# Two token groups run ahead in the opening of a two-layer mixer step on one Trainium2 core

## The chip, the core and the metric

The kernel runs on one core of one Trainium2 chip. Its five engines work side by side and wait for each other through semaphores: TensorE (PE; its weight loads are listed as PEld), VectorE (DVE), ScalarE (ACT), GpSimd (POOL) and SyncE (SP), which issues the transfers. The metric is the time of one execution on the device, in microseconds (us); lower is better.

## The reference

One inference step of a two-layer backbone over 1152 tokens (128 context, 1024 latent) with 1024 channels. Each layer normalises and modulates its input, multiplies it with one combined input weight, runs windowed attention and a pooling mixer beside each other, gates both, multiplies with an output weight and adds the result to the residual. Cut to what matters here:

```
silu_c, silu_ctx = silu(c), silu(c_ctx)
for l in range(2):
    shift, scale, gate = split(silu_c @ w_ada[l] + b_ada[l], 3)   # context tokens: silu_ctx
    h = rmsnorm(x) * norm_w[l] * (1 + scale) + shift
    q, k, v, ga, u, gp = split(h @ w_in[l])       # 512 128 128 512 512 512 columns
    q, k = rope(q), rope(k)                       # latent tokens alone
    a = rmsnorm(attention(q, k, v, cache)) * silu(ga)
    p = rmsnorm(pool_mixer(u)) * silu(gp)
    x = x + gate * (concat(a, p) @ w_out[l])
y = rmsnorm(x)                                    # k and v of the context are returned too
```

## The kernel before

**Layout.** Everything lies transposed: 128 channels on the partitions, tokens along the free dimension. The tokens are in three groups (g = 0, 1, 2) of 384; group 0 holds the 128 context tokens and the first 256 latent ones, which have modulations of their own, so that its modulation steps go in two parts (128 and 256 columns). `G[g]` holds a group's 8 channel blocks in fp32. `H[g]` holds the modulated input as two parts, hi and lo, whose sum is the fp32 value.

**A projection tile** (`project`, called by `job`) is 128 output columns of one group: for each of 8 channel blocks three matmuls (weight hi with H hi, weight hi with H lo, weight lo with H hi), 24 in all, into one PSUM accumulator. The weight's column is loaded raw in two halves (`wload`), ScalarE rounds it to hi and another engine subtracts to get lo (`wsplit`); the pair lies in one of two "wh" buffers, which comes free when all three groups have used it. Input columns go in the order U0 to U3 (pooling), V, K, Q0 to Q3, GP0 to GP3, GA0 to GA3; a layer's 18 columns times 3 groups come first, then the output projection.

**Order of work.** The program's queues are written by a list scheduler (`Sched`): generators stand for strands of work; each step is emitted when its inputs should be ready by a table of costs, by priority. The order on each engine is fixed when the program is built. Buffers are counted by tag (`BUFS` in SBUF, `PBUFS` in PSUM); `get` or `claim` waits for a free one, `put` gives it back.

**The opening (layer 0).** `start_loads` issues the first transfers in the order of `PLAN`: x*n* is a token group (1.57 MB), w*n* the *n*th of 8 blocks of modulation weights (1.05 MB; three buffers "wk", one of them in `R`, the others in the space of K and V), U*n* the *n*th weight column (0.52 MB). `take_x` squares the 8 blocks of a group (ScalarE, every fourth on VectorE), sums them over channels by products with a matrix of ones (32 columns wide, on four strips of the array), transposes, and gets the factor r = 1/rms, whose two small steps are on POOL (`rstd`). `rbcast` spreads it over the partitions. `mods_start` makes scale and shift of channel block k from the k-th block of modulation weights, in 32-column products too; `mods_tail` copies, transposes, adds the bias and sets the flags "mk". Then `hunit` makes H for one group and block: on VectorE with two `scalar_tensor_tensor` steps (G, then lo) around ScalarE's hi; for half of the blocks (`HPOOL` = (1, 3)) with POOL doing the multiplication and the scale-and-shift step, and VectorE only the last subtraction. These are the 24 "units" of the opening.

`main` starts `LANES` = 5 tiles at once: U0 for three groups, U1 for groups 0 and 1. Each takes its channel blocks as they become ready. When all five are done, it goes on tile by tile, beginning with U1 of group 2, and spawns the loads of the remaining modulation weights (`side`), the pooling (`pool_mix`) and the attention.

**After the opening.** `evac_u` copies a U tile into one of two buffers in `R`; U2 and U3 wait until U0 and U1 are pooled. When the last group of U3 is pooled, `pool_mix` loads the rotation tables (`cos`, `sin`) over the same space and sets the flag "cs". `rope`, called for K and Q tiles, waits for this flag with the tile still in its accumulator, then copies it to a "t" buffer, takes another "t", and frees the accumulator. There are two "acc" accumulators and five "t".

Of the kernel before, what the change touches and what calls it, by code (L numbers as in the profile page):

```python
# [251 lines left out]
class Kernel:  # L252
    BUFS = dict(t=5, s=8, rb=1, qs=2, pth=2, ptl=2, wr=2, wh=2)
# [65 lines left out]
    def make(self, tag, shape=None, dtype=F32):  # L319
        if tag in self.PBUFS:  # L320
            return self.ps.tile([P, 512], F32, name=tag, tag=tag, bufs=self.PBUFS[tag])
        shape = shape or ([P, GW] if tag in ("t", "rb") else [P, 512])
        return self.rg.tile(shape, dtype, name=tag, tag=tag, bufs=self.BUFS[tag])

# [30 lines left out]
    def wload(self, items):  # L355
        slot = 0
        for i, (src, second) in enumerate(items):
            if i < 2:
                yield self.has("wl", i)
                continue  # L360
            if second is not None:
                yield self.has("afin", second, 2)
            for h in range(2):
                if second is not None:
                    yield from self.claim("wr2")
                    raw = self.R[:, slot * 512:(slot + 1) * 512].rearrange("p (k f) -> p k f", k=4)
                    slot = (slot + 1) % 4
                    tag = "wr2"
                else:
                    raw = yield from self.get("wr", [P, 4, P])  # L370
                    tag = "wr"
                self.Q_.dma_start(raw, src[:, 4 * h:4 * h + 4, :])
                self.wraw[i, h] = raw, tag
                yield 0
            self.flag("wd", i)

    def wsplit(self, items):
        for i, (src, second) in enumerate(items):
            w = yield from self.get("wh", [P, 2, KD, P], R32)
            for h in range(2):  # L380
                yield lambda: (i, h) in self.wraw
                raw, tag = self.wraw.pop((i, h))
                yield from self.wait(raw)
                sl = slice(4 * h, 4 * h + 4)
                self.S_.copy(w[:, 0, sl, :], raw)
                yield
                eng = self.V_ if second is not None and h == 0 else self.P_
                eng.tensor_tensor(w[:, 1, sl, :], raw, w[:, 0, sl, :].bitcast(F32), op=ALU.subtract)
                self.put(tag)
            self.wtiles[i] = w  # L390
            yield

# [17 lines left out]
    def start_loads(self):  # L410
# [7 lines left out]
        for step in self.PLAN.split():  # L418
# [5 lines left out]
            elif kind == "U":  # L424
                tag = ("wr", "pth")[n]
# [67 lines left out]
    def mods_start(self):  # L493
        T_ = self.T_
        yield self.has("const")
        for k in range(KD):
# [59 lines left out]
    def rms_T(self, tiles, width, before=None, pre=None, add=None, after=None):  # L556
        own = pre is None
        if own:
            pre = yield from self.get("rb")
# [16 lines left out]
        if own:  # L576
            self.put("rb")
# [15 lines left out]
    def hunit(self, l, g, k, rb, tag, left):  # L593
# [4 lines left out]
        pool, V_ = turn in (self.HPOOL if l == 0 else self.HPOOL1), self.V_  # L598
# [33 lines left out]
    def take_x(self, g):  # L632
        yield self.has("xl", g)
        ps = yield from self.get("pst")
        for k in range(KD):
            x = self.G[g][:, k, :]
            yield from self.wait(x)
            sq = yield from self.get("t")
            if k % 4 in self.XDVE:
                self.V_.tensor_tensor(sq, x, x, op=ALU.mult)  # L640
            else:
                self.S_.activation(sq, x, AF.Square)
            yield
# [19 lines left out]
        yield from self.hcompute(0, g, r, "s")  # L663


    def project(self, i, g, korder, ready, tag="acc"):
# [3 lines left out]
        yield from self.wait(w)  # L670
        for n, k in enumerate(korder):
# [4 lines left out]
            self.T_.matmul(acc[:, 0:GW], w[:, 0, k, :], hi, start=(n == 0), stop=False)  # L676
            self.T_.matmul(acc[:, 0:GW], w[:, 0, k, :], lo, start=False, stop=False)
            self.T_.matmul(acc[:, 0:GW], w[:, 1, k, :], hi, start=False, stop=(n == KD - 1))
# [62 lines left out]
    def evac_v(self, l, g, acc):  # L741
# [3 lines left out]
        self.put("acc")  # L745
# [399 lines left out]
    def job(self, l, c, g, i, tag="acc"):  # L1145
# [4 lines left out]
        if self.left[i] == 0:  # L1150
            self.put("wh")
        if c == COL_K:
            sc.spawn(self.evac_k(l, g, acc), 0)
        elif c == COL_V:
            sc.spawn(self.evac_v(l, g, acc), 0)
# [10 lines left out]
    def main(self, order):  # L1166
# [3 lines left out]
        for l in range(DEPTH):  # L1170
# [4 lines left out]
            u0, u1 = order[0], order[1]  # L1175
            seq = [(c, g) for c in order[2:] for g in (self.GA if COL_GA <= c < COL_GA + 4 else range(NG))]
            if l == 0:
                lanes = [(u0, 0, "acc"), (u0, 1, "acc"), (u0, 2, "pv"), (u1, 0, "pv"), (u1, 1, "pst"), (u1, 2, "pst")][:self.LANES]
# [20 lines left out]
            for groups in (self.PASS1, (2,)):  # L1199
                for c in range(KD):  # L1200
# [6 lines left out]
                    self.put("wh")  # L1207
# [82 lines left out]
```

## Time and profile before

| | |
|---|---|
| time, median of 3 runs | 959.61 us (958.99 to 959.84) |
| the profiled execution's own time | 959.24 us |
| span of its profile | 957.3 us, 16029 instructions |
| mean granted TensorE clock | 0.993 |
| PE / PEld / DVE / ACT / POOL busy | 96% / 89% / 73% / 56% / 44% of the span |

The time is a little longer than the span, which runs from the first to the last instruction. Busy time of PE is modelled, so that short waits between matmuls can hide in it; the weight loads show them better.

### The profile page before, as it was taken

The numbers are of one execution on the slowest core, as the hardware profiler recorded it, in microseconds if no ns is written. First come the engines' busy times: TensorE is split into PE (matmuls) and PEld (weight loads), VectorE is DVE, ScalarE is ACT, GpSimd is POOL, SyncE is SP. The second block draws the span as 40 slices with busy tenths as digits, with TensorE's granted clock in tenths as the row PEclk, the third lists the DMA queues.
The fourth block names the chain that finished last, engine by engine and source line by source line (L and its number), as shares of the span: only waits on it lengthen the run. The fifth ranks groups of instructions, "written<-read, shape, count | busy, mean of one in ns | idle before, by whom it ended". The sixth has DMA issues, their size and how long they took to land.

```text
span 957.3 us, 16029 instructions
## 1 busy us (share of the span) xinstructions
PE 917.7 (96%) x5576; PEld 851.6 (89%) x5576; DVE 696.7 (73%) x1582; ACT 536.7 (56%) x1289; POOL 417.8 (44%) x460
## 2 busy tenths in 40 slices
PE   6899999999999999999999999999999999999995
PEld 1578778989999999899989999999998999999995
DVE  2774468877878578966697565887878878875384
ACT  5453333456767667663365434445777776864442
POOL 2752237654353343445233326874335335345231
PEclk9999999999999999999999999999999999999997
DMA  9716783001000000324452121110000000123363
GB/s 354 287 39 229 244 288 113 27 23 45 23 23 24 23 24 23 111 101 164 156 176 73 50 72 59 34 40 28 23 23 24 23 23 23 39 94 132 121 214 128
DMA packets 42561, 89.02 MB, mean 93 GB/s; under 512 B 4976, under 2 KB 7664, under 8 KB 42480
## 3 DMA queue, kind: packets, MB, share of 16 engines
q1 hardware_dynamic: 42480, 88.00, 26.9%
q8 instruction: 44, 0.72, 0.3%
q14 instruction: 37, 0.30, 0.1%
HBM read 78.28 MB, written 9.70 MB: 92 GB/s over the span
## 4 chain that ended last, share of the span: by engine, by line
PE 72%; DVE 15%; ACT 5%; issue 3%; POOL 3%; DMA 2%; POOLq 0%; SPq 0%; DVEq 0%; ACTq 0%
PE acc L137 50%; PE pst L137 10%; PE pv L137 6%; PE pst L148 6%; DVE G L111 4%; DVE H L111 3%; ACT s L111 2%; DVE t L111 2%; DMA G<-in_xT 1%; ACT t L111 1%; DVE s L111 1%; POOL t L111 1%; DVE ptl L111 1%; ACT wh L111 1%; DVE den L111 1%
## 5 line engine op out<-in xcount | busy, mean ns | idle before, releaser
L137 PE MATMUL acc<-H,wh 128*128 128x384 f32 x3672 | 698.1, 338 | 6.1 <-DVE H L111 2.9
L137 PEld LDWEIGHTS acc<-H,wh 128*128 128x128 f32 x3672 | 640.4, 188 | 27.4 <-issue 9.6
L111 POOL TENSOR_TENSOR wh<-wr,wh 128x512 fp32r<-128x512 f32 x102 | 139.1, 1376 | 153.2 <-ACT wh L111 149.6
L111 POOL TENSOR_SCALAR s<-s,den 128x512 f32<-128x512 f32 (+2 forms) x144 | 101.8, 720 | 180.4 <-DVE den L111 79.1
L111 DVE TENSOR_TENSOR ptl<-pst,pth 128x512 fp32r<-128x512 f32 x124 | 83.1, 686 | 19.9 <-ACT pth L111 11.2
L111 ACT CAST wh<-wr 128x512 fp32r<-128x512 f32 x102 | 62.2, 618 | 60.5 <-PE acc L137 46.6
L111 ACT ACTIVATE s<-s,m 128x512 f32<-128x512 f32 (+2 forms) x144 | 94.0, 655 | 3.5 <-DVE m L111 2.9
L111 DVE CUSTOM_DVE_ANT_0 s<-pst,cst 128x512 f32<-128x512 f32 (+2 forms) x144 | 84.1, 612 | 14.7 <-PE pst L137 13.4
L111 ACT CAST pth<-pst 128x512 fp32r<-128x512 f32 x124 | 69.6, 584 | 31.7 <-PE pst L148 24.1
L111 ACT ACTIVATE t<-G 128x384 f32<-128x384 f32 x96 | 48.6, 520 | 45.3 <-DVE G L111 35.8
L148 PE MATMUL pst<-cst,s 128*128 128x128 f32 x504 | 70.0, 274 | 3.9 <-POOL s L111 2.8
L148 PEld LDWEIGHTS pst<-cst,s 128*128 128x128 f32 x504 | 59.5, 140 | 9.8 <-POOL s L111 5.0
L137 PE MATMUL pst<-K,qs 128*128 128x256 f32 x272 | 68.2, 282 | 0.0
L137 PE MATMUL pst<-K,ql 128*128 128x256 f32 x272 | 68.0, 281 | 0.0
L111 ACT CAST qs<-G 64x256 fp32r<-64x256 f32 x144 | 58.2, 404 | 2.6
L111 DVE SCALAR_TENSOR_TENSOR G<-acc,mods,G 128x384 f32<-128x384 f32 (+2 forms) x64 | 31.5, 512 | 38.2 <-PE acc L137 38.0
L111 ACT COPY t<-pv 64x256 f32<-64x256 f32 x72 | 23.1, 369 | 55.2 <-PE pv L137 54.9
L137 PE MATMUL pv<-ptl,V 128*128 128x512 f32 x124 | 50.5, 414 | 3.1 <-DVE ptl L111 3.1
L137 PEld LDWEIGHTS pst<-K,ql 128*128 128x128 f32 x272 | 51.4, 189 | 1.4
L137 PEld LDWEIGHTS pst<-K,qs 128*128 128x128 f32 x272 | 51.5, 189 | 0.2
L137 PE MATMUL pv<-pth,V 128*128 128x512 f32 x124 | 49.9, 415 | 1.6 <-ACT pth L111 1.6
L111 POOL TENSOR_TENSOR t<-t,R 128x384 f32<-128x384 f32 (+1 forms) x30 | 34.2, 1143 | 25.0 <-DVE t L111 21.0
(120 smaller groups left out, 1175.2 us busy)
## 6 DMA issues: line engine op xcount, KB each, us to landing
wr<-in_wi SPq DMA_DIRECT2D x70, 256.0 KB, 2.6
s<-in_wada SPq DMA_DIRECT2D x44, 256.0 KB, 4.3
wr<-in_wo SPq DMA_DIRECT2D x32, 256.0 KB, 2.6
R<-in_wo SPq DMA_DIRECT2D x32, 256.0 KB, 3.4
wk<-in_wada SPq DMA_DIRECT2D x12, 512.0 KB, 5.7
G<-in_xT SPq DMA_DIRECT2D x6, 768.0 KB, 10.1
G<-in_xT SPq DMA_DIRECT2D x12, 384.0 KB, 4.0
xs<-G SPq DMA_DIRECT2D x12, 384.0 KB, 2.4
```

What stands on the lines that cost most here:

```text
L111: r = f(*args, **kw)
L137: self.eng.matmul(out, lhsT, rhs, start=start, stop=stop)
L148: self.eng.transpose(out, in_, ident)
```

## The change

In the opening, three columns (`FIRST` = 3) of groups 0 and 1 run first, six tiles; then the same three columns of group 2. The third column is V, so that the order of columns becomes U0, U1, V, U2, U3, K, Q, GP, GA, in both layers. The third weight column is kept in four "s" buffers of eight instead of "wh" (`wdone` gives them back), and its raw halves are loaded into "ptl". V's tile may lie in "pst" or "pv"; its copy waits for the end of the modulations.

`take_x` claims four "t" at once and waits for four squares before it issues their four products back to back; which engine makes a square is set for each group and block (`XDVE`, `XPOOL`, else ScalarE). `mods_start` waits for a whole block of modulation weights rather than for half of it. POOL makes no units of groups 0 and 1, and half of those of group 2. The weight differences of the first three columns go to VectorE (`WDVE`). The first step of `rstd` goes to VectorE everywhere. The first loads are reordered; x2 comes ahead of the last two modulation blocks. There are two "rb" buffers, and `rms_T` has a buffer "pre" of its own; in the opening `hcompute` uses "rb" instead of "s". A smaller DMA scratch makes room.

```diff
-    BUFS = dict(t=5, s=8, rb=1, qs=2, pth=2, ptl=2, wr=2, wh=2)
+    BUFS = dict(t=5, s=8, rb=2, pre=1, qs=2, pth=2, ptl=2, wr=2, wh=2)
-    LANES = 5
+    FIRST = 3
-    HPOOL, HPOOL1, TPOOL = (1, 3), (), (0, 1, 2, 3)
+    HPOOL, HPOOL1, TPOOL = ((), (), (1, 3)), (), (0, 1, 2, 3)
+    WDVE = (0, 1, 2)
-    XDVE = (3,)
-    PLAN = "w0 x0 U0 x1 x2 U1 w1 w2 w3 w4 w5 w6 w7"
+    XDVE, XPOOL = ((0, 2), (1, 3), (1,)), ((), (0,), (0, 2))
+    PLAN = "x0 w0 U0 x1 w1 U1 w2 U2 w3 w4 w5 x2 w6 w7"
...
     def wsplit(self, items):
         for i, (src, second) in enumerate(items):
-            w = yield from self.get("wh", [P, 2, KD, P], R32)
+            if 2 <= i < self.FIRST:
+                yield from self.claim("s", 4)
+                parts = [[self.make("s", [P, 4, P], R32) for h in range(2)] for part in range(2)]
+            else:
+                w = yield from self.get("wh", [P, 2, KD, P], R32)
+                parts = [[w[:, part, 4 * h:4 * h + 4, :] for h in range(2)] for part in range(2)]
...
-                eng = self.V_ if second is not None and h == 0 else self.P_
+                eng = self.V_ if i in self.WDVE or second is not None and h == 0 else self.P_
...
+    def wdone(self, i):
+
+        if 2 <= i < self.FIRST:
+            self.put("s", "s", "s", "s")
+        else:
+            self.put("wh")
...
-                tag = ("wr", "pth")[n]
+                tag = ("wr", "pth", "ptl")[n]
...
             for kk in range(KD):
-                if kk % 4 == 0:
-                    yield from self.wait(wt[:, kk])
+                if kk == 0:
+                    yield from self.wait(wt)
...
-        self.P_.tensor_scalar(r[:, 0:n], ssq[:, 0:n], 1.0 / width, EPS, op0=ALU.mult, op1=ALU.add)
+        self.V_.tensor_scalar(r[:, 0:n], ssq[:, 0:n], 1.0 / width, EPS, op0=ALU.mult, op1=ALU.add)
...
-            pre = yield from self.get("rb")
+            pre = yield from self.get("pre")
...
-        for k in range(KD):
-            x = self.G[g][:, k, :]
-            yield from self.wait(x)
-            sq = yield from self.get("t")
-            if k % 4 in self.XDVE:
-                self.V_.tensor_tensor(sq, x, x, op=ALU.mult)
-            else:
-                self.S_.activation(sq, x, AF.Square)
-            yield
-            j = k % 4
-            self.T_.matmul(ps[32 * j:32 * j + 32, 0:GW], self.ones, sq, start=(k < 4), stop=(k >= 4))
-            self.put("t")
+        for h in range(2):
+            yield from self.claim("t", 4)
+            sqs = [self.make("t") for _ in range(4)]
+            for j, sq in enumerate(sqs):
+                x = self.G[g][:, 4 * h + j, :]
+                yield from self.wait(x)
+                if j in self.XDVE[g]:
+                    self.V_.tensor_tensor(sq, x, x, op=ALU.mult)
+                elif j in self.XPOOL[g]:
+                    self.P_.tensor_tensor(sq, x, x, op=ALU.mult)
+                else:
+                    self.S_.activation(sq, x, AF.Square)
+                yield 0
+            yield from self.wait(*sqs)
+            for j, sq in enumerate(sqs):
+                self.T_.matmul(ps[32 * j:32 * j + 32, 0:GW], self.ones, sq, start=(h == 0), stop=(h == 1))
+            self.put("t", "t", "t", "t")
...
-        yield from self.hcompute(0, g, r, "s")
+        yield from self.hcompute(0, g, r)
...
-    def evac_v(self, l, g, acc):
+    def evac_v(self, l, g, acc, tag):
+        yield self.has("ms")
...
+            n0 = self.FIRST if l == 0 else 2
+            first = order[:n0]
+            rest = [(c, g) for c in order[n0:] for g in (self.GA if COL_GA <= c < COL_GA + 4 else range(NG))]
             if l == 0:
-                lanes = [(u0, 0, "acc"), (u0, 1, "acc"), (u0, 2, "pv"), (u1, 0, "pv"), (u1, 1, "pst"), (u1, 2, "pst")][:self.LANES]
+                lanes = [(first[n // 2], n % 2, tag) for n, tag in enumerate(("acc", "acc", "pv", "pv", "pst", "pst"))]
...
-                seq = [(u1, 2)][self.LANES - 5:] + seq
+                seq = [(c, 2) for c in first]
             else:
-                seq = [(u0, 0), (u0, 1), (u1, 0), (u1, 1), (u0, 2), (u1, 2)] + seq
+                seq = [(c, g) for c in first for g in (0, 1)] + [(c, 2) for c in first]
+            seq += rest
...
-        order = [COL_U + j for j in range(4)] + [COL_V, COL_K, 0, 1, 2, 3] + [COL_GP + j for j in range(4)] + [COL_GA + j for j in range(4)]
+        order = [COL_U, COL_U + 1, COL_V, COL_U + 2, COL_U + 3, COL_K, 0, 1, 2, 3] + [COL_GP + j for j in range(4)] + [COL_GA + j for j in range(4)]
...
-    nc = bacc.Bacc("TRN2", target_bir_lowering=False, num_devices=1)
+    nc = bacc.Bacc("TRN2", target_bir_lowering=False, num_devices=1, dynamic_dma_scratch_size=1024)
```

## Rows read from the trace of the kernel before

**Rows 1.** The profile page: busy time of each engine with its share of the span and its instructions.

```profile
PE 917.7 (96%) x5576; PEld 851.6 (89%) x5576; DVE 696.7 (73%) x1582; ACT 536.7 (56%) x1289; POOL 417.8 (44%) x460
```

**Rows 2.** Busy time by stretches: start and end, length, busy us of each engine (instructions), granted clock, share of the DMA engines, GB/s.

```profile
0.00:66.50 66.50, 53.27 (x331) 30.70 (x332) 38.76 (x90) 35.96 (x78) 35.65 (x45) 0.97 0.61 231
66.50:100.00 33.50, 33.50 (x198) 29.15 (x197) 17.54 (x38) 13.10 (x33) 10.54 (x18) 1.00 0.67 221
...
400.00:500.00 100.00, 98.25 (x580) 96.03 (x579) 74.47 (x153) 49.38 (x113) 38.08 (x36) 1.00 0.43 145
```

**Rows 3.** Weight loads (PEld) in 0 to 66.5 us by shape: count, busy us, mean ns, then the idle time before them and what ended it.

```profile
L137 PEld LDWEIGHTS acc<-H,wh 128*128 128x128 f32 x50 | 9.0, 196 | 1.8 <-ACT wh L111 0.6 <-DVE H L111 0.6 <-issue 0.4
L137 PEld LDWEIGHTS pv<-H,wh 128*128 128x128 f32 x48 | 8.3, 193 | 8.1 <-DVE H L111 4.6 <-issue 3.5
L137 PEld LDWEIGHTS pst<-H,wh 128*128 128x128 f32 x24 | 4.1, 188 | 0.8 <-issue 0.8
L137 PEld LDWEIGHTS pst<-t,ones 128*32 128x32 f32 x48 | 2.8, 115 | 9.6 <-ACT t L111 8.5 <-issue 0.8 <-ACT wh L111 0.2
L137 PEld LDWEIGHTS pst<-wk,sil 128*32 128x32 f32 x96 | 2.4, 116 | 9.5 <-issue 8.1 <-DMA wk<-in_wada 1.0 <-DVE hs L111 0.2
```

**Rows 4.** The order of time on TensorE: start us, us, operation, count, idle before and what ended it.

```profile
21.68 0.31 PEld L148 LDWEIGHTS pst<-cst,t 128*128 128x128 f32 x3 [0.62 <-ACT H L111]
22.16 0.14 PEld L137 LDWEIGHTS pst<-t,ones 128*32 128x32 f32 x2 [0.17 <-issue]
22.92 0.52 PEld L137 LDWEIGHTS acc<-H,wh 128*128 128x128 f32 x3 [0.62 <-ACT wh L111]
...
27.21 0.32 PEld L148 LDWEIGHTS pst<-cst,qs 128*128 128x128 f32 x2
...
39.07 0.16 PEld L137 LDWEIGHTS pst<-wk,sil 128*32 128x32 f32 x8 [0.25 <-issue]
39.64 0.47 PEld L137 LDWEIGHTS pst<-H,wh 128*128 128x128 f32 x3 [0.41 <-issue]
...
66.48 9.00 PE L137 MATMUL acc<-H,wh 128*128 128x384 f32 x51
```

**Rows 5.** The chain that ended last, in 0 to 70 us: start us, us, what the chain was in.

```profile
44.95 3.13 DVE G L111 x3
...
53.02 2.24 DVE G L111 x3
...
57.91 0.97 DVE hs L111
```

**Rows 6.** Busy time by stretches of 2 us, columns as in group 2.

```profile
46.00:48.00 2.00, 0.00 (x0) 0.00 (x0) 2.00 (x2) 0.62 (x2) 1.67 (x2) 1.00 0.06 13
...
50.00:52.00 2.00, 2.00 (x8) 1.67 (x7) 2.00 (x5) 2.00 (x5) 1.24 (x2) 0.50 0.00 0
```

**Rows 7.** VectorE: two lines of the opening by shape (count, busy us, mean ns, idle before), then four of the order of time, the last two from the second layer's beginning.

```profile
L111 DVE SCALAR_TENSOR_TENSOR G<-G,hs,s 128x384 f32<-128x384 f32 x8 | 6.5, 823 | 0.2
...
20.48 0.75 DVE L111 SCALAR_TENSOR_TENSOR G<-G,hs,s 128x128 f32<-128x128 f32 x2 [1.39 <-ACT s L111]
...
22.36 0.74 DVE L111 SCALAR_TENSOR_TENSOR H<-G,mods,H 128x128 fp32r<-128x128 f32 x2
...
490.91 0.67 DVE L111 TENSOR_TENSOR wh<-R,wh 128x512 fp32r<-128x512 f32 x1
...
516.22 2.21 DVE L111 SCALAR_TENSOR_TENSOR G<-G,hs,s 128x384 f32<-128x384 f32 x4 [2.26 <-ACT s L111]
```

**Rows 8.** POOL in 0 to 66.5 us by shape, the units' multiplication.

```profile
L111 POOL TENSOR_TENSOR G<-G,s 128x384 f32<-128x384 f32 x12 | 12.5, 1055 | 0.0
```

**Rows 9.** Busy time by stretches of 10 us, columns as in group 2; the last is GB/s.

```profile
0.00:10.00 10.00, 2.48 (x17) 0.62 (x18) 1.43 (x8) 2.76 (x6) 1.23 (x6) 1.00 0.77 275
10.00:20.00 10.00, 9.48 (x41) 2.49 (x42) 2.58 (x7) 7.00 (x17) 3.56 (x4) 1.00 1.02 413
20.00:30.00 10.00, 9.65 (x67) 4.08 (x63) 4.53 (x13) 6.73 (x15) 6.25 (x7) 1.00 1.03 406
30.00:40.00 10.00, 9.16 (x68) 6.24 (x69) 8.10 (x19) 6.14 (x15) 6.36 (x9) 1.00 0.75 284
```

**Rows 10.** Layer 0 in order of time, around U3 and K: the last copy of U3, the issue of the tables, the first copy of K, VectorE's step that waits for the tables.

```profile
107.02 0.48 ACT L111 COPY R<-acc 128x384 f32<-128x384 f32 x1
...
130.17 0.90 SPq L160 DMA_DIRECT2D R<-in_cs  x2
...
132.97 0.54 ACT L111 COPY t<-acc 128x256 f32<-128x256 f32 x2 [0.49 <-PE acc L137]
...
137.25 0.78 DVE L111 TENSOR_TENSOR t<-t,R 128x256 f32<-128x256 f32 x1 [3.42 <-DMA R<-in_cs]
```

**Rows 11.** Layer 1, the same place: the last copy of U3, the pooling's last two groups (first and last step), the issue of the tables, the copies of K's first two tiles; below them the tables' line in the list of transfers (count, KB each, median us from issue to landing).

```profile
563.32 0.47 ACT L111 COPY R<-acc 128x384 f32<-128x384 f32 x1
...
567.53 2.36 DVE L111 TENSOR_TENSOR R<-R 128x398 f32<-128x398 f32 x4
...
568.36 7.53 SPq L160 DMA_DIRECT2D R<-in_cs  x2
...
574.99 0.55 DVE L111 SCALAR_TENSOR_TENSOR t<-R 128x384 f32<-128x384 f32 x1
...
582.65 0.54 ACT L111 COPY t<-acc 128x256 f32<-128x256 f32 x2 [0.64 <-PE acc L137]
...
586.97 0.48 ACT L111 COPY t<-acc 128x384 f32<-128x384 f32 x1
...
R<-in_cs SPq DMA_DIRECT2D x2, 512.0 KB, 3.5
```

More of the change, by code (lines that the diff above doesn't have):

```diff
@@ L321, in make @@
             return self.ps.tile([P, 512], F32, name=tag, tag=tag, bufs=self.PBUFS[tag])
-        shape = shape or ([P, GW] if tag in ("t", "rb") else [P, 512])
+        shape = shape or ([P, GW] if tag in ("t", "rb", "pre") else [P, 512])
         return self.rg.tile(shape, dtype, name=tag, tag=tag, bufs=self.BUFS[tag])
@@ L357, in wload @@
         for i, (src, second) in enumerate(items):
-            if i < 2:
+            if i < self.FIRST:
                 yield self.has("wl", i)
@@ L383, in wsplit @@
                 yield from self.wait(raw)
-                sl = slice(4 * h, 4 * h + 4)
-                self.S_.copy(w[:, 0, sl, :], raw)
+                self.S_.copy(parts[0][h], raw)
                 yield
-                eng = self.V_ if second is not None and h == 0 else self.P_
-                eng.tensor_tensor(w[:, 1, sl, :], raw, w[:, 0, sl, :].bitcast(F32), op=ALU.subtract)
+                eng = self.V_ if i in self.WDVE or second is not None and h == 0 else self.P_
+                eng.tensor_tensor(parts[1][h], raw, parts[0][h].bitcast(F32), op=ALU.subtract)
                 self.put(tag)
-            self.wtiles[i] = w
+            self.wtiles[i] = parts
             yield
+    def wdone(self, i):
[3 more added lines that the diff above has]
+            self.put("wh")
     def constants(self):
@@ L576, in rms_T @@
         if own:
-            self.put("rb")
+            self.put("pre")
         yield
@@ L597, in hunit @@
         turn = (k + g) % 4
-        pool, V_ = turn in (self.HPOOL if l == 0 else self.HPOOL1), self.V_
+        pool, V_ = turn in (self.HPOOL[g] if l == 0 else self.HPOOL1), self.V_
         first = self.P_ if pool else V_
@@ L669, in project @@
         w = self.wtiles[i]
-        yield from self.wait(w)
+        yield from self.wait(*[x for part in w for x in part])
         for n, k in enumerate(korder):
@@ L675, in project @@
             yield from self.wait(hi, lo)
-            self.T_.matmul(acc[:, 0:GW], w[:, 0, k, :], hi, start=(n == 0), stop=False)
-            self.T_.matmul(acc[:, 0:GW], w[:, 0, k, :], lo, start=False, stop=False)
-            self.T_.matmul(acc[:, 0:GW], w[:, 1, k, :], hi, start=False, stop=(n == KD - 1))
+            self.T_.matmul(acc[:, 0:GW], w[0][k // 4][:, k % 4, :], hi, start=(n == 0), stop=False)
+            self.T_.matmul(acc[:, 0:GW], w[0][k // 4][:, k % 4, :], lo, start=False, stop=False)
+            self.T_.matmul(acc[:, 0:GW], w[1][k // 4][:, k % 4, :], hi, start=False, stop=(n == KD - 1))
             yield 0
@@ L744, in evac_v @@
         self.S_.copy(v, acc[:, 0:GW])
-        self.put("acc")
+        self.put(tag)
         yield
@@ L1150, in job @@
         if self.left[i] == 0:
-            self.put("wh")
+            self.wdone(i)
         if c == COL_K:
@@ L1154, in job @@
         elif c == COL_V:
-            sc.spawn(self.evac_v(l, g, acc), 0)
+            sc.spawn(self.evac_v(l, g, acc, tag), 0)
         elif c < 4:
@@ L1174, in main @@
             i += len(order)
-            u0, u1 = order[0], order[1]
-            seq = [(c, g) for c in order[2:] for g in (self.GA if COL_GA <= c < COL_GA + 4 else range(NG))]
+            n0 = self.FIRST if l == 0 else 2
+            first = order[:n0]
+            rest = [(c, g) for c in order[n0:] for g in (self.GA if COL_GA <= c < COL_GA + 4 else range(NG))]
             if l == 0:
-                lanes = [(u0, 0, "acc"), (u0, 1, "acc"), (u0, 2, "pv"), (u1, 0, "pv"), (u1, 1, "pst"), (u1, 2, "pst")][:self.LANES]
+                lanes = [(first[n // 2], n % 2, tag) for n, tag in enumerate(("acc", "acc", "pv", "pv", "pst", "pst"))]
                 for n, (c, g, tag) in enumerate(lanes):
@@ L1206, in main @@
                         yield 0
-                    self.put("wh")
+                    self.wdone(i)
                     i += 1
```

## The prediction

> **What bounds the kernel now.** I read four views in turn. The page first: TensorE is busy 96% of the span and its weight loads 89%, the next engine, VectorE, 73% [rows 1]. Then busy time by stretches: from 66.5 us on TensorE has hardly a gap (98.25 us of 100 in the middle of the kernel, 33.50 of 33.50 right behind the opening), but in the first 66.5 us it is busy for 53.27 us and its loads for only 30.70 [rows 2]. So a microsecond won before 66.5 us moves everything behind it, if nothing new stops TensorE later.
>
> Third, what the opening contains. The loads of projection matmuls in it are 50 + 48 + 24 = 122 [rows 3], that is 5 output tiles (24 matmuls each: 8 contraction blocks, 3 products) and 2 matmuls. A matmul in an undisturbed run takes 9.00 us / 51 = 0.1765 us [rows 4], so these tiles are 21.5 us of work. The rest of the opening is squares, modulation products, small transposes and waits: the loads of the squares waited 9.6 us, those of the modulations 9.5 us and those of tiles in "pv" 8.1 us, 4.6 of it for VectorE's H [rows 3]. The first projection load comes at 22.92 us [rows 4].
>
> Fourth, the chain of waits inside the opening. It runs over VectorE: three steps for G of 3.13 us at 44.95, three of 2.24 us at 53.02, and the last scale vector at 57.91, 0.97 us for a 2-column instruction [rows 5]. All three groups' modulations, 24 units, have to pass before the five tiles can end, and 12 of them use POOL (12 multiplications, 12.5 us [rows 8]); beside POOL's work VectorE's 384-column G step takes 823 ns on average [rows 7], while four in a row in the second layer take 2.21 us, 0.55 each [rows 7]. At 46:48 TensorE did nothing, and at 50:52 its clock was 0.50 [rows 6].
>
> **Part by part: projections.** Before, the opening ends with 5 tiles. In the change six tiles (first three columns, groups 0 and 1) need only 16 units, and the three tiles of group 2 follow. I compare the time at which 9 tiles are done. Before, with the opening's other work done too, that is 66.5 us plus 4 tiles: 96 x 0.1765 = 16.9, so 83.4 us.
>
> *TensorE's work up to there in the change.* Nine tiles: 216 x 0.1765 = 38.1 us. A modulation visit of 8 loads costs 0.25 us to enter and 0.57 us from its first load to the next operation's (39.07 to 39.64) [rows 4]. Of the 0.57, some 0.43 is the product itself (the array works as four strips of 32 columns here, each with two loads' worth of 256 columns). With 16 loads in one visit I take 0.25 + 0.57 + 0.43 = 1.25 us as an estimate; two visits cost 1.64, so each block that is split now gives back 0.4 us. With a block's two transposes (0.32 us of loads at 27.21 [rows 4]) eight blocks make 12.5 us. A square visit of 2 loads costs 0.76 us (22.16 to 22.92) [rows 4]; one with four squares side by side, a strip each, adds loads only, so I estimate 1.0 us: six visits, 6.0 us, for up to 24 before. Three chains from squares to the broadcast factor: two triples of transposes each, 0.31 us of loads a triple (21.68 [rows 4]), 1.9 us. Together 58.5 us.
>
> *How early it can start.* The loads bring 2.75 MB in the first 10 us and 0.41 MB a microsecond after that [rows 9]. In the new order (a token group 1.57 MB, a modulation block 1.05, a weight tile 0.52) x0 is there at 7.1 us, the first modulation block at 9.7, U0 at 11.0, x1 at 14.8, the second block at 17.4, U1 at 18.6, the third block at 21.2, U2 at 22.5, x2 at 34, the last block at 39. By 25 us TensorE can have done four square visits (4.0), three modulation blocks (4.7), two chains (1.2) and some 24 projections (4.2): 14.1 us. What is left, 44.4 us, then runs from 25 us: 69.4 us at the earliest. That is the lower bound. Waits of the kind seen before come on top: 4.6 us for H [rows 3], and about 1.5 us for a stretch at half clock [rows 6]. That is 75.5 us; gain 83.4 - 75.5 = 8 us. With twice these waits it is 81.6 us and 2 us; without any, 14 us.
>
> *Does VectorE keep up?* A group-0 unit is two split pairs, 0.75 + 0.74 us [rows 7]: 8 x 1.49 = 11.9. Group 1: 8 x 1.1 = 8.8. Group 2, half with POOL's help: 4 x 1.1 + 4 x 0.55 = 6.6. The six weight differences now on VectorE (0.67 us each at 490.91 [rows 7]): 4.0. Ten squares (0.55): 5.5. Modulation tails, three small instructions, 0.64 each estimated from the undisturbed ones: 5.1. Reductions and the scale step that moves from POOL: about 1. In all 43 us, from 7 us on: 50 us if never idle, some 55 with first waits. That is before TensorE's 75 less two tiles, 67. If all 384-column G and H steps kept 823 ns it would be some 10 us more, 65: still just in time. So POOL's cover gone costs nothing that I count.
>
> *The late x2 stands ahead of the last two modulation blocks:* they come 3.9 us later than without it. TensorE has a backlog at 35 us by the working above, so this is hidden; if not, it costs up to 3.9 us, in the range. The waits for a whole modulation block rather than half cost at most 1.3 us, once, at the first.
>
> **Part by part: what follows.** V now comes ahead of U2, U3, and K directly behind U3, in both layers. This is the part that can cost. K's rotation needs the tables loaded over the pool buffers once U3 is pooled. Before, three V tiles lay between. *Layer 1:* U3's last copy is at 563.32, the pooling of the last two groups begins at 567.53 and its last step ends at 574.99 + 0.55, 8.0 us [rows 11]; the tables take a few us to land, 3.5 in the transfer list [rows 11]. So after the change the tables are there about 11.5 us behind U3's last copy and are issued at 8.0. K's tiles come at 4.4 and 8.8 us; the third, in the accumulator freed at about 8.5, at 13.2. The accumulator of the second is free only when the first rotation has returned its buffers: with tables present 4.3 us separate the two copies (582.65 to 586.97) [rows 11], of which I count 3.4 behind the tables: 14.9. Stall 14.9 - 13.2 = 1.7 us. *Layer 0:* here modulation work lies between tiles: three V tiles and the first K tile lie between 107.02 and 132.97, 6 us a tile and more [rows 10], so K's third tile ends at about 18 us and the stall is nil. The upper bound is that the pooling is as late as it is now: tables issued at 130.17, 23 us behind 107.02 [rows 10]. TensorE would then stop after two K tiles, at 12, until 23: 11 us. I take 2 us for both layers, nearer to the pooling's own rows than to its waits.
>
> The second "rb" buffer, the own "pre" buffer and the scale step on VectorE shorten chains that TensorE hardly waits for behind the opening: 0 to 1 us gained, taken as 0. The four "s" buffers held by the third weight tile can delay the second half of the adaLN loads; these fill gaps on TensorE and are not due until the output projection: 0, and up to 2 us if a filler is missing.
>
> **Sum.** The profiled execution: 959.24 us, span 957.3. 959.2 - 8 + 2 = 953.2; the median is 0.4 above that execution, so **953.6 us**.
>
> **Rivals.**
> *The table wait takes the place (slower).* For it: K's first copy now comes only 2.8 us behind the issue of the tables (130.17, 132.97), and VectorE waited 3.42 us for their landing [rows 10]. Against: much of the 23 us is idle time between pooling steps. With today's lags layer 0 stalls 11 us and layer 1, where the tables' second half is issued by 575.9, 12.6 behind the copy [rows 11], 12.6 - 8.8 = 3.8 and the rotation's 2: 17 in all, against a gain of 8: 968 us. It decides from a stall of 8 us on. Chance 0.14.
> *The two cancel, or the opening gains nothing:* TensorE's first 25 us stay as thin as they are and waits for H double (gain 2), stalls 2: about 959.5. For it: VectorE is as full as before, 43 us against 38.76 [rows 2]. Chance 0.13.
> *The clock falls in the thin start.* The trace holds it at 1.00 in the first two 10 us stretches although loads were busy 0.62 and 2.49 us of them [rows 9], and has it at 0.50 behind the idle 46:48 [rows 6]. If the 14.1 us of work of the first 25 us ran at half the clock, it would take 28.2, 3.2 us too long: 956.8. Chance 0.06. [...]
> *A full gain,* 69.4 us reached: 14 us, 947. Chance 0.07.
>
> **How the numbers follow.** The forecast itself, gain 3 to 10 us, has 0.60. Faster by over 0.2% (1.9 us, about what a measurement of this kernel can tell) is forecast, full gain and clock: 0.73. Same 0.13, slower 0.14. The range leaves out most of the slower case and the end of the full gain: 946 to 961. The likeliest case alone spans 949.5 to 957.
>
> **What the changed profile would show.** First projection load near 15 us instead of 22.92; 216 projection loads done at 75 us (now 83.4); VectorE's G steps near 0.55 us in the opening; square visits of 8 loads, modulation visits of 16. If the ninth tile ends after 80 us, the opening term is wrong; if K's copies wait for the tables with an idle TensorE of over 3 us near 125 or 580 us, the second term is.

## The result and the profile after

The changed kernel takes 971.99 us (median of 4 runs, 970.33 to 974.52) beside 959.30 us for the kernel before: ratio 1.0136, 95% interval 1.0112 to 1.0161. It is slower by 13 us where 6 us less were forecast. The profiled execution took 972.32 us, its span is 970.5 us.

The page of the kernel after, busy time by engine and then the granted clock in 40 slices:

```profile
PE 919.0 (95%) x5576; PEld 853.9 (88%) x5576; DVE 710.6 (73%) x1629; ACT 533.1 (55%) x1279; POOL 404.2 (42%) x419
...
PEclk9999999999999999999999999999999999999998
```

TensorE's work is nearly the same (919.0 us against 917.7, [rows 1]); of the 13.2 us that the span grew, nearly all is idle time. Busy time by stretches of the kernel after, columns as in [rows 2]:

```profile
0.00:66.50 66.50, 52.40 (x357) 34.86 (x357) 43.61 (x114) 31.41 (x68) 17.02 (x21) 1.00 0.63 239
66.50:100.00 33.50, 31.31 (x182) 27.06 (x183) 22.51 (x41) 14.79 (x35) 11.63 (x16) 1.00 0.53 173
...
500.00:600.00 100.00, 93.07 (x528) 90.64 (x527) 62.84 (x119) 42.20 (x94) 32.18 (x38) 0.99 0.19 64
600.00:700.00 100.00, 95.27 (x560) 90.67 (x560) 83.42 (x199) 54.86 (x147) 61.36 (x65) 0.97 0.09 30
```

The opening does hold more loads, 357 instead of 332 [rows 2]. But the stretch right behind it has 2.2 us of idle time that was not there (31.31 of 33.50), and 500:700 has 11.7 us, where the kernel before has 3.1:

```profile
500.00:600.00 100.00, 98.57 (x571) 97.39 (x570) 66.24 (x130) 46.85 (x104) 40.44 (x48) 1.00 0.19 64
600.00:700.00 100.00, 98.34 (x607) 94.96 (x606) 83.17 (x208) 58.48 (x159) 57.20 (x63) 1.00 0.09 30
```

**A view that finds the place.** Two kernels with the same matmuls in another order can be laid beside each other by work done: I count TensorE's weight loads in stretches of 10 us, give each kind a fixed time (0.1765 us for a projection matmul), add up, and read when each kernel reaches the same sum. The table is worked out in this way, not a view of the profile: us ahead (-) or behind (+) the kernel before, at the time of the kernel before in the first column. The other columns are the kernels of the experiments below. At the end the table can be held against the spans: there it is off by up to 1.7 us (18.6 for e2, whose span is 974.2 us against 957.3), so smaller differences in it say little.

```
before  after    e1    e2    e3    e9   e17   e12   e16
  65.1   -6.4  -7.4  +0.8  -7.9  -6.6  +0.3  +0.4  -4.1
  85.9   -2.1  -2.9  +1.0  -3.3  -4.4  +0.4  +0.7  -3.6
 129.0   -0.6  -1.9  +4.1  -2.6  -5.0  +3.1  +0.8  -4.9
 193.7   -1.8  -2.6  +9.3  -3.1  -4.4  +1.3  -0.0  -4.9
 526.0   -0.1  +0.3  +9.9  -0.8  -3.5  -1.9  +0.8  -3.6
 604.7   +8.0  +0.7 +17.6  +5.9  +0.4  +1.8  +1.2  -2.8
 665.7  +13.7  +1.3 +18.4  +8.2  +1.8  +4.7  +0.9  -2.4
 856.3  +12.1  +1.5 +18.0  +6.3  -1.8  +4.5  -3.8  -1.6
 934.0  +12.9  +1.6 +18.6  +7.2  -2.0  +4.5  -3.1  -1.6
```

The changed kernel is 6.4 us ahead at 65 us. It loses most of that by 86 us, nearly all the rest by 129 us, runs level to 526 us, and falls 13 us behind between 526 and 666 us, in layer 1.

**The place in layer 1.** The order of time of the kernel after: the last copy of U3, the tables' issue, the copy of K's first tile, two of VectorE's steps of its rotation (the first needs the tables), three steps of ScalarE up to the copy of K's second tile, and TensorE's matmuls.

```profile
579.94 0.48 ACT L111 COPY R<-acc 128x384 f32<-128x384 f32 x1
...
583.43 5.87 SPq L160 DMA_DIRECT2D R<-in_cs  x2
...
589.46 0.53 ACT L111 COPY t<-acc 128x256 f32<-128x256 f32 x2
...
592.67 0.43 DVE L111 TENSOR_TENSOR t<-t,R 128x256 f32<-128x256 f32 x1 [2.15 <-DMA R<-in_cs]
593.20 0.42 DVE L111 TENSOR_TENSOR t<-t 128x256 f32<-128x256 f32 x1
595.09 0.62 ACT L111 CAST wh<-wr 128x512 fp32r<-128x512 f32 x1 [3.11 <-PE acc L137]
595.62 1.03 ACT L111 CAST K<-t 64x384 fp32r<-64x384 f32 x2
...
596.67 0.48 ACT L111 COPY t<-acc 128x384 f32<-128x384 f32 x1
...
597.20 6.00 PE L137 MATMUL acc<-H,wh 128*128 128x384 f32 x24 [2.19 <-ACT t L111]
...
603.43 4.46 PE L137 MATMUL acc<-H,wh 128*128 128x384 f32 x24 [0.23 <-ACT t L111]
...
608.71 3.59 PE L137 MATMUL acc<-H,wh 128*128 128x384 f32 x19 [0.82 <-ACT G L111]
```

K's second copy comes 16.7 us behind U3's last copy. The first tile's rotation holds its "t" buffers until the tables have landed; VectorE uses them at 592.67 and is through at 593.62. ScalarE's queue adds 2.0 us to that: in front of the rounding of K (595.62) it has the rounding of a next weight (595.09), which waited 3.11 us for TensorE's products. TensorE has filled both accumulators and waits 2.19 us for the copy. So part of this wait is a circle, TensorE waiting for ScalarE that waited for TensorE: with K's rounding and the copy directly behind 593.62 the copy would have ended near 595.2 (an estimate from these rows), and TensorE stopped at 595.0. Then TensorE's granted clock is low (0.64 in 598:600, 0.51 in 600:602): 24 matmuls take 6.00 us instead of 4.46 in the next tile. In [rows 11] the first two copies of K were 19.3 and 23.7 us behind U3's, with V in between, and the tables long there. In layer 0 of the kernel after the tables are issued at 129.70, 6.7 us behind U3's copy at 123.01, and K's second copy comes 9.3 us behind the first, instead of 7.4 in the kernel before (132.97 [rows 10] to 140.33, the last line here):

```profile
123.01 0.47 ACT L111 COPY R<-acc 128x384 f32<-128x384 f32 x1
...
130.43 0.54 ACT L111 COPY t<-acc 128x256 f32<-128x256 f32 x2 [0.60 <-PE acc L137]
...
136.33 0.68 DVE L111 TENSOR_TENSOR t<-t,R 128x256 f32<-128x256 f32 x1 [3.78 <-DMA R<-in_cs]
...
139.74 0.48 ACT L111 COPY t<-acc 128x384 f32<-128x384 f32 x1
```

```profile
140.33 0.48 ACT L111 COPY t<-acc 128x384 f32<-128x384 f32 x1
```

Here TensorE has modulation products to do, and little waiting shows: from 100 to 160 us its longest wait is 1.2 us.

### The profile page after: what moved, and what is told of

Its sections match the earlier page's. It is cut to its first block, busy times and chain, and to the rows that moved or that the text cites. A ratio compares the mean times of both kernels' runs of the same rounds, so it can differ in the third digit from the quotient of the medians.

```text
span 970.5 us, 15980 instructions
## 1 busy us (share of the span) xinstructions
PE 919.0 (95%) x5576; PEld 853.9 (88%) x5576; DVE 710.6 (73%) x1629; ACT 533.1 (55%) x1279; POOL 404.2 (42%) x419
## 4 chain that ended last, share of the span: by engine, by line
PE 69%; DVE 18%; issue 5%; POOL 3%; ACT 3%; DMA 1%; SPq 0%; POOLq 0%; DVEq 0%; ACTq 0%
PE acc L137 46%; PE pst L137 10%; PE pst L148 7%; PE pv L137 6%; DVE G L111 5%; DVE H L111 3%; DVE t L111 2%; DVE R L111 2%; DVE s L111 2%; ACT s L111 1%; DVE ql L111 1%; DMA G<-in_xT 1%; POOL wh L111 1%; DVE den L111 1%; POOL t L111 1%
## 5 line engine op out<-in xcount | busy, mean ns | idle before, releaser
L137 PE MATMUL acc<-H,wh 128*128 128x384 f32 x3624 | 689.9, 339 | 16.2 <-DVE H L111 9.8
L137 PEld LDWEIGHTS acc<-H,wh 128*128 128x128 f32 x3624 | 633.1, 189 | 42.9 <-DVE H L111 12.2
L111 POOL TENSOR_TENSOR wh<-wr,wh 128x512 fp32r<-128x512 f32 x98 | 134.6, 1386 | 174.3 <-ACT wh L111 165.9
L111 POOL TENSOR_SCALAR s<-s,den 128x512 f32<-128x512 f32 (+2 forms) x144 | 105.3, 746 | 140.3 <-DVE den L111 76.9
L111 DVE CUSTOM_DVE_ANT_0 s<-pst,cst 128x512 f32<-128x512 f32 (+2 forms) x144 | 84.5, 613 | 13.3 <-PE pst L137 12.7
L111 ACT ACTIVATE t<-G 128x384 f32<-128x384 f32 x86 | 43.7, 520 | 44.0 <-DVE G L111 28.1
L111 DVE TENSOR_TENSOR R<-R 128x384 f32<-128x384 f32 (+13 forms) x60 | 43.3, 722 | 25.9 <-ACT R L111 24.5
L111 POOL TENSOR_TENSOR rr<-rr,nhalf 128x3 f32<-128x3 f32 x21 | 21.5, 1026 | 68.6 <-DVE rr L111 68.3
```

The source lines that it names most:

```text
L111: r = f(*args, **kw)
L137: self.eng.matmul(out, lhsT, rhs, start=start, stop=stop)
```

## The experiments

Theory A: the order of columns is the loss, because K directly behind U3 waits for the rotation tables. Rival B: the buffers and the rest of the scheduling are, and layer 1 is chance. Rival C: the gap that V leaves in the feeding of the pooling, between U1 and U2. Later: theories D and E, on why the opening's lead is lost.

**e1: the old order in layer 1 alone.**

```diff
-        order = [COL_U, COL_U + 1, COL_V, COL_U + 2, COL_U + 3, COL_K, 0, 1, 2, 3] + ...
+        orders = [[COL_U, COL_U + 1, COL_V, COL_U + 2, COL_U + 3, COL_K, 0, 1, 2, 3] + last,
+                  [COL_U, COL_U + 1, COL_U + 2, COL_U + 3, COL_V, COL_K, 0, 1, 2, 3] + last]
```

> The changed kernel with the old order of columns in layer 1 alone (U0 U1 U2 U3 V K Q...); layer 0 and the opening stay as changed. Theory A (layer 1's order is the loss: K directly behind U3 waits for the rotation tables): the 13 us that the changed kernel falls behind between 510 and 670 us are gone, 958 to 960.5 us. Rival B (the loss comes from the buffers and the other scheduling of the change, and shows in layer 1 by chance): 966 us or more.

Measured: 961.20 us, ratio 1.0020 (1.0011 to 1.0029). Of the 12.7 us lost, 10.8 are layer 1's order; B falls. It lies 0.7 us above what A gave: about 0.2% stays lost elsewhere.

**e2: the order alone, in the kernel before.**

```diff
-        order = [COL_U + j for j in range(4)] + [COL_V, COL_K, 0, 1, 2, 3] + ...
+        order = [COL_U, COL_U + 1, COL_V, COL_U + 2, COL_U + 3, COL_K, 0, 1, 2, 3] + ...
```

> The kernel before with nothing but the new order of columns (U0 U1 V U2 U3 K Q...) in both layers; opening, buffers and loads stay as before. Theory A: layer 1 loses its 13 us here too, 970 to 975 us, and layer 0 a little, since modulation work lies between its tiles there. Rival B: within 2 us of before, 957 to 962.

Measured: 975.71 us, ratio 1.0166 (1.0152 to 1.0180), 0.7 us above what A gave. The order alone costs 16 us, more than the whole change: 9 us in layer 0 (by 194 us) and 8 more between 526 and 605. So the rest of the change is worth some 4 us, and layer 0, where I had expected a little, loses as much as layer 1.

**e3: K directly behind U3 in layer 1, V behind K.** (The changed kernel with `U0 U1 U2 U3 K V Q...` in layer 1.)

> The changed kernel with U0 U1 U2 U3 K V Q... in layer 1: pooling is fed without a gap as before, but K stays directly behind U3. If the distance from U3 to K is the loss (theory A), 967 to 973 us. If the gap that V leaves in the feeding of the pooling between U1 and U2 is the loss (rival C), 958 to 962 us.

Measured: 967.24 us, ratio 1.0085 (1.0066 to 1.0104): 6.0 us above e1. The distance from U3 to K costs by itself, and what is missing to the changed kernel, 4.8 us, comes with V ahead of U2. Waits of TensorE in 555 to 612 us of this kernel (us in total, times, longest):

```profile
PE acc L137 <- ACT t L111: 5.1, 3, 2.2
```

These are the copies of K and Q tiles that come late; in the same stretch of e1 there is no such line.

**e4: two columns in the opening, the old order.** `FIRST = 2`, `WDVE = (0, 1)`, no U2 in `PLAN`, four lanes, and the old `order`.

> The changed kernel with two columns in the opening (four tiles of groups 0 and 1, then U0 and U1 of group 2) and the old order of columns in both layers; squares, modulation visits, load order, buffers as changed. If the rewritten opening gives its lead without V as a third column: 954 to 957.5 us. If what the opening wins is given back behind it whatever the order (the changed kernel led by 6 us at 60 us and by under 1 us at 130): 958.5 to 960.5.

Measured: 963.79 us, ratio 1.0046 (1.0033 to 1.0058). Both ranges were missed. With four tiles instead of six TensorE's loads wait for H: 3.2 us on VectorE and 2.0 us on ScalarE in 57 to 90 us. In this run the new opening has no lead without its third column; counted as in the table, it is 1 to 2 us behind at 65 us and 4 to 5 at 86.

**e9: the wait taken away.** The changed kernel, its order in both layers, with the tables in a buffer of their own that is loaded once.

```diff
+        self.T2 = cp.tile([P, 2 * LAT], F32, name="T2")
-        self.cos = self.R[:, 0:LAT]
-        self.sin = self.R[:, LAT:2 * LAT]
+        self.cos = self.T2[:, 0:LAT]
+        self.sin = self.T2[:, LAT:2 * LAT]
...
         yield self.has("h", l, 2, 0)
+        if l == 0:
+            self.Q_.dma_start(self.cos, self.a["cs"][0])
+            self.Q_.dma_start(self.sin, self.a["cs"][1])
+        self.flag("cs", l)
         for j in range(4):
...
-        self.Q_.dma_start(self.cos, self.a["cs"][0])
-        self.Q_.dma_start(self.sin, self.a["cs"][1])
-        self.flag("cs", l)
```

> The changed kernel, its order of columns in both layers, but with the rotation tables in a buffer of their own that is loaded once, when the pooling of layer 0 begins; no K tile waits for the pooling of U3 any more. Theory A (K's wait for tables is what layer 1 loses when K follows U3): the part of layer 1's loss that belongs to K behind U3 goes, that is some 6 us and what follows from it, 960 to 966 us. Rival C (the gap in the pooling and a crowd behind it is what costs, on TensorE's own queue): 968 to 972 us.

Measured: 956.22 us, ratio 0.9970 (0.9957 to 0.9984): faster than before, and 15.8 us below the changed kernel. Both ranges were missed. It is more than A expected, since layer 0 gains too: by the table the lead at 129 us is 5.0 instead of 0.6. Not all of that is the wait. At 86 us, ahead of any K tile, 2.3 us of it are there already, because the list scheduler wrote another order: in the kernel after, products of the pooling stand in TensorE's queue before their inputs are ready (first two lines); in e9 they come later in the work and wait for nothing (third line).

```profile
76.56 0.44 PE L137 MATMUL pst<-pth,s 128*128 128x384 f32 x1 [1.02 <-ACT pth L111]
77.67 0.44 PE L137 MATMUL pst<-ptl,s 128*128 128x384 f32 x1 [0.67 <-DVE ptl L111]
```

```profile
78.06 0.34 PE L137 MATMUL pst<-pth,s 128*128 128x384 f32 x1
```

The place in layer 1 (U3's last copy, K's first two copies), without a wait of TensorE for either:

```profile
574.47 0.48 ACT L111 COPY R<-acc 128x384 f32<-128x384 f32 x1
578.06 0.54 ACT L111 COPY t<-acc 128x256 f32<-128x256 f32 x2 [2.18 <-PE acc L137]
585.70 0.48 ACT L111 COPY t<-acc 128x384 f32<-128x384 f32 x1
```

K's first copy is 3.6 us behind U3's last, instead of 9.5.

**e10: tables apart and the old order in layer 1** (e1 with the edit of e9).

> The changed kernel with the old order in layer 1 and with the tables in a buffer of their own, loaded once. With the old order three V tiles cover the wait already: 959.5 to 962 us, no change from the same kernel with the tables over the pool buffers (961.2). If layer 0 still waits for its tables, up to 2 us less.

Measured: 956.38 us, ratio 0.9976 (0.9965 to 0.9987). Between e9 and e10, without the wait, the order in layer 1 makes no difference in the time. The expectation was missed: I had left layer 0 at most 2 us, and the tables were worth 4.8 (961.20 to 956.38). Here too a part is there ahead of K: by 85 us TensorE has begun 232 loads of projections, 221 in e1.

**e11: tables apart in the kernel before** (the edit of e9, with the smaller DMA scratch for room).

> The kernel before with the tables in a buffer of their own, loaded once when the pooling of layer 0 begins (the smaller DMA scratch makes room). In the trace of before K's first copy came 2.8 us behind the issue of the tables and VectorE waited 3.4 us for them, with TensorE busy all the while. If three V tiles cover the wait: 958 to 960, and the 3 us that the changed kernel with tables apart is below before belong to the opening and the rest of the change. If before waits for tables too: 955 to 957, and the change itself brings nothing.

Measured: 959.09 us, ratio 0.9998 (0.9988 to 1.0007). In the kernel before, three V tiles covered the wait completely. Nothing of the cover shows in the profile of before; without it, the next run says, the wait costs 12.5 us.

**e17: the order alone, tables apart** (e2 with the edit of e9).

> The kernel before with the new order of columns in both layers and the tables in a buffer of their own: the order alone, without its wait for the tables. The order alone cost 16 us (975.7). Theory A (all of it is the wait for the tables): 958 to 961 us. If part of it is the gap that V leaves in the feeding of the pooling: 963 to 968.

Measured: 963.20 us, ratio 1.0042 (1.0028 to 1.0056). Of the order's 16 us the wait for the tables is 12.5 (975.71 to 963.20). Up to 86 us these two kernels are level in the table within 0.6 us, so this is the cleaner price of the wait. The other 3.8 lie in layer 1 (5 us behind from 666 us on, after a small lead), where the pooling is fed late: VectorE's step for U2 in this kernel follows 6.67 us of idle time behind the V tiles.

```profile
556.79 1.81 DVE L111 TENSOR_TENSOR R<-R 128x406 f32<-128x406 f32 x3 [6.67 <-ACT R L111]
```

That this gap is the reason is argued, not shown: e9 has the same 6.67 us and is no slower than e10, which has no such gap. By the table e9 loses 5.3 us from 526 to 666 us and wins 3.6 back by 856 us.

**Why the opening's lead shrinks: e5, e7, e13, e14.** In the kernel after the chain of group 2 is late. Its squares begin at 36.05, on POOL; the factor's first step stands behind other work on VectorE until 56.65, 2.6 us after its input (54.03); then VectorE and POOL make G side by side, four steps each, in 5.37 and 4.91 us.

```profile
36.05 3.09 POOL L111 TENSOR_TENSOR t<-G 128x384 f32<-128x384 f32 x3 [12.43 <-DMA G<-in_xT]
...
54.03 0.17 DVE L111 TENSOR_REDUCE ssq<-pst 128x3 f32<-128x12 f32 x1
...
56.65 0.16 DVE L111 TENSOR_SCALAR rr<-ssq 128x3 f32<-128x3 f32 x1
...
59.54 5.37 DVE L111 SCALAR_TENSOR_TENSOR G<-G,hs,rb 128x384 f32<-128x384 f32 x4 [0.31 <-ACT rb L111]
59.58 4.91 POOL L111 TENSOR_TENSOR G<-G,rb 128x384 f32<-128x384 f32 x4 [1.81 <-ACT rb L111]
```

*e5* (on e1): `PLAN` with x2 ahead of w3.

> The changed kernel with the old order in layer 1, and the third token group loaded ahead of the fourth to eighth modulation block instead of ahead of the last two. Theory D (the opening's lead of 7 us at 60 us is lost until 90 us because group 2's H comes late, at 59 to 71 us, and crowds VectorE with the pooling): H of group 2 is ready earlier, the lead at 90 us grows from 3 to about 5 us, 958 to 960 us. If the modulation blocks, now 4 us later, set the pace: the lead at 60 us shrinks by up to 4 us and the time is 961 to 964.

Measured: 959.79 us, ratio 1.0003 (0.9990 to 1.0015). The lead at 65 us shrinks from 7.4 to 3.3 us, as the expectation said for the case that the modulation blocks set the pace; D's larger lead at 86 us does not come (1.8). The time, though, lies in D's range, 1.4 us below e1's with intervals that overlap: undecided.

*e7* (on e1): `rstd`'s first step on POOL again.

> The changed kernel with the old order in layer 1, and the first step of rstd on POOL again. In the opening this step of group 2 stood 2.6 us behind its input in VectorE's queue (54.03 and 56.65). If that wait is on the path of group 2's H: 959 to 960.5 us. If the step costs nothing on either engine: 961 to 962.

Measured: 964.75 us, ratio 1.0057 (1.0039 to 1.0076): 3.5 us slower than e1, where I had expected a gain or nothing. The lead at 65 us falls to 0.7; why the step is worth so much was not followed further.

*e12*: the kernel before with that one step on VectorE.

```diff
-        self.P_.tensor_scalar(r[:, 0:n], ssq[:, 0:n], 1.0 / width, EPS, op0=ALU.mult, op1=ALU.add)
+        self.V_.tensor_scalar(r[:, 0:n], ssq[:, 0:n], 1.0 / width, EPS, op0=ALU.mult, op1=ALU.add)
```

> The kernel before with the first step of rstd on VectorE instead of POOL, nothing else. Undoing it in the changed kernel with the old layer-1 order cost 3.5 us. If the step as such is worth that: 955 to 957 us. If it is worth it only beside POOL's squares in the new opening: 958.5 to 960.

Measured: 955.42 us, ratio 0.9960 (0.9945 to 0.9975). One line is worth 3.8 us. By the table it has brought nothing up to 666 us; the gain comes in layer 1's attention. TensorE's loads there, 690 to 860 us, waited 3.1 us for "pth" and 2.9 for "ptl" before (first two lines); in e12 the wait for "ptl" is gone and the list is the last two:

```profile
PEld pv L137 <- ACT pth L111: 3.1, 6, 0.9
PEld pv L137 <- DVE ptl L111: 2.9, 2, 1.9
```

```profile
PEld pv L137 <- ACT pth L111: 1.5, 3, 0.9
PEld pst L148 <- POOL s L111: 0.5, 2, 0.3
```

Neither of these is the chain that the step stands in. The list scheduler wrote another order there, and whether the gain is the step's or that order's is left open. It bears on the changed kernel as well: e9 lies 3.0 us below the kernel before, no more than this one step brings there. So no run shows that the opening's lead is worth anything at the end; a kernel with the new opening, the tables apart and this step on POOL would have to.

*e13* (on e9): `HPOOL` empty for group 2 too.

> The changed kernel with tables apart, and no POOL in the units of group 2 either: VectorE makes all of them. In the changed kernel four G steps of group 2 took 5.37 us beside POOL's 4.91 us (59.5 to 65), 1.34 each instead of 0.55. Theory E (the two engines hold each other up there): group 2's H is ready some 3 us earlier, more of the opening's lead survives, 953 to 955.5 us. If VectorE is the bound all the same: 956 to 957.5.

Measured: 956.61 us, ratio 0.9967 (0.9954 to 0.9980), in the second range. The two engines did hold each other up: VectorE's eight G steps of group 2 now take 4.33 us, 0.54 each, instead of 1.34.

```profile
59.74 4.33 DVE L111 SCALAR_TENSOR_TENSOR G<-G,hs,rb 128x384 f32<-128x384 f32 x8 [0.31 <-ACT rb L111]
```

The lead at 86 us grows from 4.4 to 5.6 us; the end does not move.

*e14* (on e9): `PLAN` with x2 behind w3.

> The changed kernel with tables apart, and the third token group loaded behind the fourth modulation block (before, behind the sixth; ahead of the fourth it left the time the same within the interval). If group 2's chain is what ends the opening: 954 to 955.5 us. If the modulation blocks pace it: 956.5 to 959.

Measured: 958.16 us over a wide spread (954.38 to 960.33), ratio 0.9986 (0.9971 to 1.0001): inconclusive. D is not borne out: neither place of x2 moved the end by more than the noise.

**e16: all but layer 1's order.** e10 with the edit of e13.

> The changed kernel with tables apart, no POOL in the units of group 2, and the old order in layer 1. With the new order this kernel led by 4.7 us at 565 us and was 1.5 us behind at 646, then ended 2.3 ahead. If the order still costs there without the table wait: the lead of 5 us stays to the end, 952.5 to 954.5 us. If the lead is lost again in the attention of layer 1 whatever the order: 956 to 957.

Measured: 954.80 us, ratio 0.9951 (0.9938 to 0.9965), the lowest ratio of all, but its interval overlaps that of e12, where one line was moved. It lies between the two expectations. By the table it stays 3.6 us ahead through 526 us and keeps 1.6 at the end; a loss of 2 us is hardly more than the table can tell.

## Why the prediction was wrong

- **The step that failed** is the second term, the stall of K behind U3, put at 2 us for both layers. Taking the wait away is worth 12.5 us in the kernel with the old opening (e2 to e17) and 15.8 us in the changed one (971.99 to 956.22, e9), of which some 2 us come from another order of TensorE's queue ahead of K. The mechanism was named, with its place; its size in the sum was wrong. A rival with a chance of 0.14 gave 968 us for it, but that is in part luck: it had 11 us of stall in layer 0 and 6 in layer 1, where the trace has no wait of TensorE over 1.2 us around K in layer 0, and layer 1's order cost 10.8 us (e1).
- **Layer 1.** The steps themselves came near: tables issued 9.4 us behind U3's copy (583.43 + 5.87) where I said 8.0, used at 12.7 for 11.5, K's second copy at 16.7 for 14.9, TensorE's wait 2.19 us for 1.7. ScalarE's queue, which made part of that wait, was not in the forecast. I stopped there, and so did my sign for this term, an idle TensorE of over 3 us at K's copies. Behind it came 24 matmuls at the low clock (1.5 us more than the next tile), waits of 0.23 and 0.82 us for the next copies, and a late start of the attention with a second stretch at a low clock (0.52 in 636:638): 8 us behind at 605 us, 13.7 at 666. With the wait gone the same stretch, 526 to 666 us, loses 5.3 instead of 13.8 us.
- **Layer 0.** "The stall is nil, modulation work lies between" was wrong: up to 4.8 us (e1 against e10), part of it ahead of K. That work did keep TensorE busy then, but it was not extra work: done early, it is missing later. I infer this from the table; no run shows it by itself.
- **The opening** failed as a term too: put at 8 us, it brought 2.1 by its own measure, the time at which 216 projection loads are done. The last of them begins at 84.72 us, in the kernel before at 86.84, not at the 83.4 that I worked out: there I left out the pooling and modulation products between the tiles. The forecast's sign, a ninth tile that ends after 80 us, is there. Loads of projections begun by 85 us, before and after (busy us and count):

```profile
0.00:85.00 85.00, 35.95 (x207) 0.98 0.62 228
```

```profile
0.00:85.00 85.00, 36.86 (x217) 1.00 0.58 216
```

- **Where the opening's lead went.** It is 6.4 us at 65 us and 2.1 at 86, and the first projection load comes at 20.61 us, not 15 (operations that take longer in the start, last section, may have a part in that; no run prices it). Two steps failed here. One is "VectorE keeps up": its total was about right (43.61 us busy in the first 66.5, I had 43), but I asked only whether the sum fits and not when group 2's chain gets its turn. POOL's first square of x2 begins at 36.05 us, near my 34 for its landing; the factor is spread at 59.02 us, 23 us later. The other is the 0.55 us for a 384-column G step: the twelve of the opening took 0.87 us on average, and by e13 the 1.34 us of group 2's four come from POOL working beside them.
- **"Taken as 0"** for `rstd` was wrong by about 3.5 us, in the kernel's favour (e7, e12).
- **Right:** what is lost behind 66.5 us is idle time of TensorE; square visits of 8 loads and modulation visits of 16 are there (0.85 us at 43.73 and 1.07 at 21.82, where the kernel before took 0.83 for 2 loads at 22.16 and 0.64 for 8 at 36.20); the old kernel's cover was complete (e11).

## What to carry to other kernels

When a change moves work away from between two dependent steps, price the wait as if no cover were left, and follow it to the next stage, not to the first stall: the first stall was 2.2 us, the loss 12.5 to 15.8. A wait that costs nothing in the profile of before can still be the reason why the order is as it is; look for it at every place where a buffer is reused for something else. Where the wait exists only because two things share space, giving them each their own can be cheaper than ordering around it (956.2 us against 972.0). An opening's lead is not yet a gain: the 6.4 us at 65 us were 2.1 at 86, and at the end no run shows more than one moved step brings by itself. And where a list scheduler writes the queues, an edit in one place changes the order in others, so the price of a wait is best taken from a pair of runs that is level up to it.

## What the runs showed of the hardware

The granted clock is shown as 1.00 from the start, but the same operations take longer there than later. In the kernel after, three transposes' loads took 0.66 us at 14.93 and 0.30 at 23.67; one block of modulation products took 1.93 us at 12.23 and 1.07 at 21.82. The kernel before began so too: a modulation product took 633 ns on average in the first block, from 6.08 us on, and 391 ns in 30 to 46 us.

```profile
14.93 0.66 PEld L148 LDWEIGHTS pst<-cst,rr 128*128 128x128 f32 x3
...
23.67 0.30 PEld L148 LDWEIGHTS pst<-cst,rr 128*128 128x128 f32 x3
```

That is 1.6 to 2.2 times the later duration. Whether a low clock is the cause is not shown: the column has 1.00 in both places. So the forecast's rival of a low clock in the thin start is left open by these runs.

In layer 1 the granted clock was low behind two of TensorE's waits: one of 2.19 us up to 597.20 (0.64 in 598:600, 0.51 in 600:602) and one of 1.72 us up to 634.80, where it waited for POOL (0.52 in 636:638, 0.62 in 638:640). The stretches 590:600, 600:610 and 630:640 of the kernel after have it at 0.93, 0.90 and 0.83; the first two of e9 have it at 1.00.

```profile
590.00:600.00 10.00, 7.77 (x39) 7.45 (x40) 4.08 (x10) 4.11 (x8) 4.14 (x4) 0.93 0.25 83
600.00:610.00 10.00, 8.95 (x44) 8.31 (x44) 7.69 (x15) 4.48 (x10) 3.85 (x4) 0.90 0.08 26
630.00:640.00 10.00, 8.26 (x40) 7.61 (x39) 7.58 (x17) 5.01 (x15) 7.31 (x9) 0.83 0.15 54
```
